# A decoder layer's Z stage fed from x in two layouts: four unscaled fp32 products, column weight and root in one VectorE pass

## The chip, the cores and the metric

The kernel runs on one core of a Trainium2 chip. The metric is the device time of one execution in microseconds (us). PE is TensorE, DVE is VectorE, ACT is ScalarE, POOL is GpSimd, SP is SyncE, which issues most of the DMAs.

## The reference, cut to what matters

One decoder layer on x of 1024 tokens by 1024 columns: an RMS norm, one input projection split into a differential attention group and a gated DeltaNet group, an output projection, and a squared-ReLU MLP. The change lies in the first stage, which computes the norm and the columns of the projection that feed the gate (z) and the decay and write strength (a, b) of the DeltaNet group:

```python
h = rms_norm(x, norm1_w[l])        # x * rsqrt(mean(x*x) + EPS) * w, row by row
proj = h @ w_in[l]
da_q, da_k, da_v, dn_qkv, dn_z, dn_a, dn_b = jnp.split(proj, [...], axis=-1)
...
dn_o = rms_norm(dn_o, dn_out_norm_w[l]) * jax.nn.silu(dn_z.reshape(B, S, DN_HEADS, DN_V_DIM))
```

The later projections use the same h, so the stage also leaves h behind for them.

## The kernel before, in words

**Tiles.** The 1024 tokens are eight blocks of 128, `tb` = 0 to 7. TensorE contracts over partitions, so h is wanted with its columns on partitions: `hH` and `hL` hold h transposed, as eight column blocks `k` of 128 by 1024 tokens. `hH` is h rounded to fp32r and `hL` is what is left, h - hH. The weights are split in the same way (`wH`, `wL`; `z_round` on ACT, `z_rest` on DVE). A product in this split form (`z_mm`, lines 290 to 292) is three matmuls for each `k`: hH wH, hH wL, hL wH, so 24 for one token block and one unit. The Z weights are two units `u` of 260 columns; unit 0 is gate columns, unit 1 is 252 gate columns and the 8 columns of a and b. So the stage has 16 products.

**One block before.** x is loaded as rows (tokens on partitions). ACT squares a block and sums each row (`z_square`, L321); `z_root` takes the root (DVE L223, then a power on POOL, L224); `z_scale` (DVE, L335) multiplies the rows by root and column weight `w1b`; PE transposes the eight column blocks (`z_turn`, L340); ACT copies the result into `hH` (`h_round`, L345) and DVE writes `hL` (`h_rest`, L349). `z_gate` takes a finished product out of PSUM: tanh on ACT (L298), a pass on DVE (L300), a multiplication by `dn_out_norm_w` on POOL (L301), and a store. For block 0 and unit 0 the product is made in plain fp32 from the copied transposes `hF` (L388), before the split forms exist.

`w1b`, the column weight on all partitions, is made by PE from one row (L362).

**What sets the order.** The stage stands in `tc.manual_schedule`: the engines named there take their instructions in the order of the program, each engine for itself. Before, these are PE, DVE and ACT. What stands outside that block (constants, loads, the projections behind it) is placed by a scheduler; the lines between `mark` and `behind.close()` are held behind instructions of the iteration `tb == 3` and behind the last load of x. SP issues the loads.

**Behind the stage** come the DeltaNet projections (`dn_proj`, PE lines 198 to 200). Their weight buffers `wH` and `wL` are those of the Z units, so the first of them is split when the last product of unit 0 is done.

Of the kernel before, what the change touches and what calls it, by code (L numbers as in the profile page):

```python
# [18 lines left out]
P = 128  # L19
# [9 lines left out]
UC = 260  # L29
# [91 lines left out]
def tile_hymba_layer(  # L121
    ctx: ExitStack,
    tc: tile.TileContext,
    x, norm1_w, w_z, w_units, lambda_q1, lambda_k1, lambda_q2, lambda_k2, q_norm_w, k_norm_w,
# [128 lines left out]
    w1b = n1.tile([P, DM], F32, name="w1b")  # L253

    def z_unit(u):

        ops = [staged(t).rearrange("p (k c) -> p k c", k=KB) for t in ("wH", "wL")]
        raws = []
        for k in range(0, KB, 2):
            raw = n1.tile([P, 2 * UC], F32, tag="wraw", name="wraw", bufs=8)  # L260
            nc.sync.dma_start(raw, w_z[u, k // 2, :, 0:2 * UC])
            raws.append(raw.rearrange("p (k c) -> p k c", k=2))
        return ops, raws

    xts = [n1.tile([P, DM], F32, tag="xt", name="xt", bufs=NT) for _ in range(NT)]
    hF = n1.tile([P, KB, P], F32, name="hF")
    w1r = hF.rearrange("p k c -> p (k c)")[0:1, :]
    nc.scalar.dma_start(w1r, norm1_w)
    cuts = (slice(0, 512), slice(512, 1024))
    for c in cuts:  # L270
        nc.sync.dma_start(xts[0][:, c], x2[0:P, c])
    nc.sync.dma_start(xts[1], x2[P:2 * P, :])
    wz = [z_unit(u) for u in range(2)]
    dnw4 = n1.tile([P, 4, P], F32, name="dnw4")
    nc.sync.dma_start(dnw4[:, 0], dn_out_norm_w.partition_broadcast(P))
    for tb in range(2, NT):
        x_last = nc.sync.dma_start(xts[tb], x2[tb * P:(tb + 1) * P, :])
    G.tensor_scalar(dnw4[:, 0], dnw4[:, 0], 0.5, None, ALU.mult)
    G.tensor_copy(dnw4[:, 1:4], dnw4[:, 0:1].broadcast_to([P, 3, P]))
    dnw4 = dnw4.rearrange("p h e -> p (h e)")  # L280

    def z_mm(tb, u, pool=pj, tag="pj", mid=None):
# [4 lines left out]
        for k in range(KB):  # L287
            if k == 2 and mid:
                mid()
            T.matmul(ps[:, :UC], hH[:, k, sl], wh[:, k, :], start=k == 0, stop=False)  # L290
            T.matmul(ps[:, :UC], hH[:, k, sl], wl[:, k, :], start=False, stop=False)
            T.matmul(ps[:, :UC], hL[:, k, sl], wh[:, k, :], start=False, stop=k == KB - 1)
        return ps

    def z_gate(tb, u, ps):
        n = UC if u == 0 else 252
        th = n1.tile([P, UC], F32, tag="zth", name="zth", bufs=2)
        S.activation(th[:, :n], ps[:, :n], AF.Tanh, scale=0.5)  # L298
        zg = n1.tile([P, UC], F32, tag="zg", name="zg", bufs=4)
        last = V.scalar_tensor_tensor(zg[:, :n], th[:, :n], 1.0, ps[:, :n], ALU.add, ALU.mult)  # L300
        G.tensor_tensor(zg[:, :n], zg[:, :n], dnw4[:, UC * u:UC * u + n], ALU.mult)  # L301
        if u == 1:
            last = V.tensor_copy(ab[:, tb, :], ps[:, 252:260])
# [10 lines left out]
    hns_, turned_ = {}, {}  # L314

    def z_square(tb, parts=1):
        hn = n1.tile([P, DM], F32, tag="hn", name="hn", bufs=2)
        ss = n1.tile([P, 2], F32, tag="nss", name="nss", bufs=2)
        for i in range(parts):
            c = cuts[i] if parts > 1 else slice(0, DM)  # L320
            S.activation(hn[:, c], xts[tb][:, c], AF.Square, accum_out=ss[:, i:i + 1])  # L321
        hns_[tb] = hn, ss

    def z_root(tb, parts=1):

        hn, ss = hns_[tb]
        if parts > 1:
            V.tensor_tensor(ss[:, 0:1], ss[:, 0:1], ss[:, 1:2], ALU.add)
        r = n1.tile([P, 1], F32, tag="nr", name="nr", bufs=2)
        rstd(r, ss[:, 0:1], 1.0 / DM, EPS, n1, "nrt", 1)  # L330
        hns_[tb] = hn, r

    def z_scale(tb, c):
        hn, r = hns_[tb]
        return V.scalar_tensor_tensor(hn[:, c], xts[tb][:, c], r, w1b[:, c], ALU.mult, ALU.mult)  # L335

    def z_turn(tb, g):
        ps = pt_.tile([P, 512], F32, tag="pt", name="ps_tr")
        for j in range(4 * g, 4 * g + 4):
            last = T.transpose(ps[:, (j % 4) * P:(j % 4 + 1) * P], hns_[tb][0][:, j * P:(j + 1) * P], ident)  # L340
        turned_[tb, g] = ps.rearrange("p (k t) -> p k t", k=4)
        return last

    def h_round(tb, g):
        return S.copy(hH[:, 4 * g:4 * g + 4, tb * P:(tb + 1) * P], turned_[tb, g])  # L345

    def h_rest(tb, g):
        ks, sl = slice(4 * g, 4 * g + 4), slice(tb * P, (tb + 1) * P)
        V.tensor_tensor(hL[:, ks, sl], turned_[tb, g], hH[:, ks, sl].bitcast(F32), ALU.subtract)  # L349

    ones = gp.tile([P, P], F32, name="ones")
    with tc.manual_schedule(engines={T.engine, V.engine, S.engine}):


        V.memset(ones, 1.0)
        pw = pm.tile([P, 512], F32, tag="pm", name="ps_w")
        for i in range(6):
            T.transpose(pw[:, 0:P], ident, ident)
        pws = []
        for c in cuts:  # L360
            ps = ph.tile([P, 512], F32, tag="ph", name="ps_w1")
            T.matmul(ps, ones[0:1, :], w1r[:, c], start=True, stop=True)  # L362
            pws.append(ps)
        for i in range(6):
            T.transpose(pw[:, 0:P], ident, ident)
        V.tensor_copy(w1b[:, cuts[0]], pws[0])
        z_square(0, 2)
        z_root(0, 2)
        V.tensor_copy(w1b[:, cuts[1]], pws[1])
        z_square(1)  # L370
        for g in range(2):
            z_scale(0, cuts[g])
            z_turn(0, g)
        z_round(0, 0)
        z_root(1)
        S.copy(hF[:, 0:4, :], turned_[0, 0])
        z_rest(0, 0)
        z_round(0, 1)
        S.copy(hF[:, 4:8, :], turned_[0, 1])
        z_scale(1, slice(0, DM))  # L380

        ps = pj.tile([P, 512], F32, tag="pj", name="ps_z")
        banks0 = {0: ps}
        for k in range(KB):
            if k == 4:
                z_turn(1, 0)
                z_turn(1, 1)
            T.matmul(ps[:, :UC], hF[:, k, :], wz[0][1][k // 2][:, k % 2, :], start=k == 0, stop=k == KB - 1)  # L388
        for i in (2, 3):
            z_round(0, i)  # L390
        for i in (1, 2, 3):
            z_rest(0, i)
        for g in range(2):
            h_round(1, g)
            h_rest(1, g)
        for i in range(2):
            z_round(1, i)
            z_rest(1, i)
        for g in range(2):
            ks = slice(4 * g, 4 * g + 4)  # L400
            S.copy(hH[:, ks, 0:P], hF[:, ks, :])
            V.tensor_tensor(hL[:, ks, 0:P], hF[:, ks, :], hH[:, ks, 0:P].bitcast(F32), ALU.subtract)
            z_round(1, 2 + g)
            z_rest(1, 2 + g)
        z_square(2)
        z_root(2)
        banks0[1] = z_mm(1, 0)
        z_gate(0, 0, banks0[0])
        z_scale(2, slice(0, DM))
        z_square(3)  # L410
        banks0[2] = z_mm(0, 1, ph, "ph")
        z_gate(1, 0, banks0[1])
        z_root(3)
        banks0[3] = z_mm(1, 1, ph, "ph", lambda: (z_turn(2, 0), z_turn(2, 1)))
        for g in range(2):
            h_round(2, g)
            h_rest(2, g)
        z_gate(0, 1, banks0[2])
        z_scale(3, slice(0, DM))
        z_gate(1, 1, banks0[3])  # L420
        for tb in range(2, NT):
            ps = z_mm(tb, 0)
            if tb + 1 < NT:
                marks = [z_turn(tb + 1, 0), z_turn(tb + 1, 1)][1:]
                for g in range(2):
                    marks += [h_round(tb + 1, g)]
                    h_rest(tb + 1, g)
            marks += [z_gate(tb, 0, ps)]
            if tb + 2 < NT:
                z_square(tb + 2)  # L430
                z_root(tb + 2)
                z_scale(tb + 2, slice(0, DM))
            if tb == 3:
                mark = marks
            ps = z_mm(tb, 1)
            z_gate(tb, 1, ps)
# [3 lines left out]
    for ins in mark + [x_last]:  # L440
# [3 lines left out]
    tri = sp.tile([P, P], F32, name="tri")  # L444
    G.affine_select(tri, ones, pattern=[[1, P]], compare_op=ALU.is_ge, fill=0.0,
                    base=0, channel_multiplier=-1)
    gt_f = gp.tile([P, P], F32, name="gt_f")
    G.affine_select(gt_f, ones, pattern=[[-1, P]], compare_op=ALU.is_gt, fill=0.0,
                    base=0, channel_multiplier=1)
    gt_r = gp.tile([P, P], F32R, name="gt_r")  # L450
    V.tensor_copy(gt_r, gt_f)
    blk = gp.tile([P, P], F32, name="blk")
    G.affine_select(blk.rearrange("p (b c) -> p b c", c=32), ones.rearrange("p (b c) -> p b c", c=32),
                    pattern=[[-32, 4], [0, 32]], compare_op=ALU.is_ge, fill=0.0,
                    base=-32, channel_multiplier=1)
    caus_f = gp.tile([P, P], F32, name="caus_f")
    G.memset(caus_f, 0.0)
    G.affine_select(caus_f, caus_f, pattern=[[-1, P]], compare_op=ALU.is_ge, fill=-1.0e30,
                    base=0, channel_multiplier=1)
# [103 lines left out]
    def dn_proj(kind):  # L563
        for pr in range(2):
            w = load_unit(w_units[6 + 2 * kind + pr])
# [1223 lines left out]
```

## Time and profile before

| | |
|---|---|
| median of 3 runs | 1257.38 us (1255.05 to 1257.84) |
| the profiled execution | 1254.91 us, span of its instructions 1253.2 us |
| granted TensorE clock, mean | 0.997 |
| busy in the span | PE 98%, its weight loads 85%, DVE 65%, ACT 49%, POOL 9% |
| Z stage on PE | from the first product at 10.02 us to the first projection at 63.45 us |

The durations that the prediction uses come from the profiled execution. In a row of the timeline the first number is the start in us from the span's start, the second the duration in us, then engine, line, operation, tiles written and read, shapes and the count. A bracket gives the idle time of that engine just before, and what ended it. In a row of windows, after the bounds and the length, stand the busy time and the number of instructions of PE, PEld, DVE, ACT and POOL, then the granted clock, the share of the DMA engines and GB/s. Durations overlap with the next instruction on the same engine, so prices are taken from start to start.

### The profile page before, as it was taken

The page shows a single profiled execution, that of the slowest core. Times are in us where ns is not written, and L with a number is a line of the kernel's source. Part 1 is how long each engine was busy: PE and PEld are TensorE (multiplying, and loading weights), DVE is VectorE, ACT ScalarE, POOL GpSimd, SP SyncE. Part 2 cuts the span into 40 slices and gives each one's busy share as a digit, 9 for nine tenths or more (in the row PEclk, how much of TensorE's full clock was granted, in tenths as well). Part 3 has the DMA queues.
Part 4 walks back from the last instruction along what each step waited for, and adds up shares of the span by engine and source line. Part 5 has one row for each costly group of instructions (what it writes and reads, how often), then busy time and mean ns, then how long its engine had stood idle before and what let it go on. Part 6 is the DMA issues. An engine that isn't in the chain of part 4 may idle for free.

```text
span 1253.2 us, 18946 instructions
## 1 busy us (share of the span) xinstructions
PE 1232.7 (98%) x6965; PEld 1061.6 (85%) x6965; DVE 817.7 (65%) x1416; ACT 612.5 (49%) x1239; POOL 111.4 (9%) x143
## 2 busy tenths in 40 slices
PE   9999999999998999999999999999999999999998
PEld 8978888899998998787888888888888888888887
DVE  6567797656556647776589555655569855787553
ACT  5378553334345545656567445445564333333331
POOL 3311110022112200001200000000000000000000
PEclk9999999999999999999999999999999999999999
DMA  7134554368758557322255544443469655422301
GB/s 245 43 102 129 160 159 113 89 215 240 249 144 243 157 176 180 97 66 80 85 185 172 201 159 175 168 152 132 170 219 376 230 199 201 168 101 101 133 35 67
DMA packets 156343, 197.93 MB, mean 158 GB/s; under 512 B 20650, under 2 KB 110554, under 8 KB 156251
## 3 DMA queue, kind: packets, MB, share of 16 engines
q1 hardware_dynamic: 156248, 196.72, 48.4%
q8 instruction: 55, 0.90, 0.3%
q14 instruction: 38, 0.30, 0.1%
q10 hardware_dynamic: 2, 0.00, 0.0%
HBM read 131.66 MB, written 65.01 MB: 157 GB/s over the span
## 4 chain that ended last, share of the span: by engine, by line
PE 91%; DMA 4%; DVE 2%; ACT 2%; issue 1%; SPq 0%; DVEq 0%; POOL 0%; ACTq 0%; POOLq 0%
PE X L1391 5%; PE X L1392 5%; PE X L1393 5%; PE X L1691 4%; PE X L1690 4%; PE X L1689 4%; PE ps_dn L198 3%; PE ps_dn L199 3%; PE ps_dn L200 3%; PE ps_qk L955 3%; PE ps_qk L957 3%; PE ps_qk L956 3%; PE Y L1391 2%; PE Y L1392 2%; PE Y L1393 2%; PE ps_op L1220 2%
## 5 line engine op out<-in xcount | busy, mean ns | idle before, releaser
L1309 ACT CAST hH<-ur 128x1024 fp32r<-128x1024 f32 x56 | 58.9, 1051 | 173.3 <-PE Y L1690 89.8
L1310 DVE TENSOR_TENSOR hL<-ur,hH 128x1024 fp32r<-128x1024 f32 x56 | 68.3, 1223 | 79.9 <-ACT hH L1309 79.8
L955 PE MATMUL ps_qk<-wH,hH 128*128 128x256 f32 x384 | 115.5, 301 | 0.1
L957 PE MATMUL ps_qk<-wH,hL 128*128 128x256 f32 x384 | 109.1, 284 | 0.0
L956 PE MATMUL ps_qk<-wL,hH 128*128 128x256 f32 x384 | 109.0, 284 | 0.0
L1310 DVE TENSOR_TENSOR op<-raw,op 128x1024 fp32r<-128x1024 f32 x48 | 58.7, 1223 | 74.5 <-PE X L1392 41.5
L1689 PE MATMUL X<-hH 128*128 128x512 f32 x224 | 87.1, 389 | 0.0
L1690 PE MATMUL X<-hL,hH 128*128 128x512 f32 x224 | 87.1, 389 | 0.0
L1691 PE MATMUL X<-hH,hL 128*128 128x512 f32 x224 | 87.1, 389 | 0.0
L198 PE MATMUL ps_dn<-hH,wH 128*128 128x512 f32 x192 | 76.1, 397 | 0.3 <-ACT cp L574 0.3
L200 PE MATMUL ps_dn<-hH,wL 128*128 128x512 f32 x192 | 75.9, 396 | 0.0
L199 PE MATMUL ps_dn<-hL,wH 128*128 128x512 f32 x192 | 75.7, 395 | 0.0
L955 PEld LDWEIGHTS ps_qk<-wH,hH 128*128 128x128 f32 x384 | 74.0, 193 | 0.3 <-ACT qn L974 0.2
L956 PEld LDWEIGHTS ps_qk<-wL,hH 128*128 128x128 f32 x384 | 74.0, 193 | 0.0
L957 PEld LDWEIGHTS ps_qk<-wH,hL 128*128 128x128 f32 x384 | 73.8, 192 | 0.0
L193 DVE TENSOR_TENSOR wL<-wraw,wH 128x512 fp32r<-128x512 f32 x64 | 43.9, 697 | 37.9 <-ACT wH L192 37.7
L1310 DVE TENSOR_TENSOR hL<-dw,hH 128x1024 fp32r<-128x1024 f32 x56 | 68.1, 1219 | 0.5 <-ACT hH L1309 0.5
L1309 ACT CAST op<-raw 128x1024 fp32r<-128x1024 f32 x48 | 50.4, 1051 | 35.3 <-PE Y L1393 19.9
L1309 ACT CAST hH<-dw 128x1024 fp32r<-128x1024 f32 x56 | 58.7, 1048 | 10.1 <-DMA dw<-in_w_down_dram 4.4
L192 ACT CAST wH<-wraw 128x512 fp32r<-128x512 f32 x64 | 38.2, 620 | 48.7 <-DMA wraw<-in_w_units_dram 35.3
L578 DVE SCALAR_TENSOR_TENSOR cy<-cp,pv,cy 128x512 f32<-128x512 f32 x72 | 53.7, 747 | 7.2 <-ACT cy L576 6.4
L1080 DVE TENSOR_REDUCE mx<-ps_sc 128x1 f32<-128x128 f32 (+7 forms) x64 | 47.6, 754 | 15.3 <-PE ps_sc L1078 14.8
(366 smaller groups left out, 3451.3 us busy)
## 6 DMA issues: line engine op xcount, KB each, us to landing
ur<-ud SPq DMA_DIRECT2D x28, 1024.0 KB, 4.9
raw<-in_w_up_dram SPq DMA_DIRECT2D x32, 512.0 KB, 4.1
dw<-in_w_down_dram SPq DMA_DIRECT2D x32, 512.0 KB, 6.6
wraw<-in_w_units_dram SPq DMA_DIRECT2D x48, 256.0 KB, 3.9
qk_d<-qa SPq DMA_DIRECT2D x32, 256.0 KB, 3.6
ud<-ua SPq DMA_DIRECT2D x16, 512.0 KB, 3.3
ud<-s SPq DMA_DIRECT2D x16, 512.0 KB, 2.7
pka<-park_d SPq DMA_DIRECT2D x32, 192.0 KB, 3.7
```

Of the source, the lines that this page charges most:

```text
L198: T.matmul(ps, lh(k), rh(k), start=(k == 0), stop=False)
L199: T.matmul(ps, lh(k), rl(k), start=False, stop=False)
L200: T.matmul(ps, ll(k), rh(k), start=False, stop=(k == n - 1))
L955: T.matmul(ps[:, :256], hH[:, k, sl], wh[:, k, :], start=(k == 0), stop=False)
L956: T.matmul(ps[:, :256], hH[:, k, sl], wl[:, k, :], start=False, stop=False)
L957: T.matmul(ps[:, :256], hL[:, k, sl], wh[:, k, :], start=False, stop=(k == KB - 1))
L1309: S.copy(dst[0], src)
L1310: V.tensor_tensor(dst[1], src, dst[0].bitcast(F32), ALU.subtract)
L1391: T.matmul(ps, op[0][:, k, cs], h[0][:, k, :], start=start and k == 0, stop=False, skip_group_check=True)
L1689: T.matmul(bank[t], v[0][:, j, sl], v[2][:, j], start=s0, stop=False, skip_group_check=True)
L1690: T.matmul(bank[t], v[0][:, j, sl], v[3][:, j], start=False, stop=False, skip_group_check=True)
L1691: T.matmul(bank[t], v[1][:, j, sl], v[2][:, j], start=False, stop=s1, skip_group_check=True)
```

## The change: what it does

- **x comes in two layouts.** The host hands over `x_cols`, where each token block already has columns on partitions, beside x itself. Each block is loaded twice: as `xT` for the products, and as rows `xt` for the squares alone. The transposes on PE are gone.
- **Four unscaled products.** The products of blocks 0 and 1 with both units are made in plain fp32 from `xT` times the column weight (`z_weigh`, then `z_raw`), without the root. Their root is applied in `z_gate`: as the scale of the tanh, and in an additional DVE pass which also takes the place of the POOL multiplication.
- **The root is spread by PE.** ACT scales the identity by a block's roots (`z_diag`), and PE multiplies ones by that diagonal (`z_spread`), so that each partition holds the roots of all 128 tokens. `z_spread` stands inside a product, ahead of column block `at`.
- **Column weight and root in one DVE pass.** `z_scale` multiplies `xT` by the column weight and the spread roots, straight from PSUM, in eight passes of 128x128 (blocks 2 to 7) or two of 128x512 with the roots alone (blocks 0 and 1, weighted before), then writes `hH` and `hL`. Blocks 0 and 1 get theirs late, in the iterations 4 and 5.
- **Order.** Loads and roots are reordered; POOL is now also in manual order, its masks ahead of the stage. The first loads of the projections' weights stand behind the last load of x.

The diff, cut to its core:

```diff
+    def z_raw(tb, u, pool, tag, mid=None, at=2):
+        ps = pool.tile([P, 512], F32, tag=tag, name="ps_z")
+        for k in range(KB):
+            if k == at and mid is not None:
+                z_spread(mid)
+            T.matmul(ps[:, :UC], xTs[tb][:, k, :], wz[u][1][k // 2][:, k % 2, :], start=k == 0, stop=k == KB - 1)
+        return ps
...
-        S.activation(th[:, :n], ps[:, :n], AF.Tanh, scale=0.5)
+        S.activation(th[:, :n], ps[:, :n], AF.Tanh, scale=half_r[tb] if raw else 0.5)
         last = V.scalar_tensor_tensor(zg[:, :n], th[:, :n], 1.0, ps[:, :n], ALU.add, ALU.mult)
-        G.tensor_tensor(zg[:, :n], zg[:, :n], dnw4[:, UC * u:UC * u + n], ALU.mult)
+        if raw:
+            last = V.scalar_tensor_tensor(zg[:, :n], zg[:, :n], r, w, ALU.mult, ALU.mult)
+        else:
+            G.tensor_tensor(zg[:, :n], zg[:, :n], w, ALU.mult)
...
+    def z_weigh(tb):
+        for c in cuts:
+            V.tensor_tensor(xTs[tb][:, c, :], xTs[tb][:, c, :], w1c[:, c].unsqueeze(2).broadcast_to([P, 4, P]),
+                            ALU.mult)
+    def z_diag(tb):
+        diags[tb] = n1.tile([P, P], F32, tag="dg", name="dg", bufs=4)
+        S.activation(diags[tb], ident, AF.Copy, scale=roots[tb])
+    def z_spread(tb):
+        ps = pm.tile([P, 512], F32, tag="pm", name="ps_r")
+        marks[tb] = T.matmul(ps[:, :P], ones, diags[tb], start=True, stop=True)
+        spreads[tb] = ps[:, :P]
+    def z_scale_parts(tb):
+        sl = slice(tb * P, (tb + 1) * P)
+        xT, last = xTs[tb], []
+        for c in cuts:
+            if tb < 2:
+                V.tensor_tensor(xT[:, c, :], xT[:, c, :], spreads[tb].unsqueeze(1).broadcast_to([P, 4, P]), ALU.mult)
+            else:
+                for k in range(c.start, c.stop):
+                    V.scalar_tensor_tensor(xT[:, k, :], xT[:, k, :], w1c[:, k:k + 1], spreads[tb], ALU.mult, ALU.mult)
+            last.append(S.copy(hH[:, c, sl], xT[:, c, :]))
+        yield
+        for c in cuts:
+            last.append(V.tensor_tensor(hL[:, c, sl], xT[:, c, :], hH[:, c, sl].bitcast(F32), ALU.subtract))
+        yield last
...
+        z_weigh(0)
+        z = {(0, 0): z_raw(0, 0, pj, "pj")}
+        for i in range(3):
             z_round(0, i)
             z_rest(0, i)
+        z_weigh(1)
+        z_round(0, 3)
+        z_rest(0, 3)
+        z[1, 0] = z_raw(1, 0, pj, "pj")
+        for i in range(4):
             z_round(1, i)
             z_rest(1, i)
         z_square(2)
         z_root(2)
+        z_diag(2)
+        z[0, 1] = z_raw(0, 1, ph, "ph", 2, 6)
         z_square(3)
         z_root(3)
+        z_diag(3)
+        z[1, 1] = z_raw(1, 1, ph, "ph", 3, 4)
+        z_scale(2)
+        z_square(0)
+        z_square(1)
+        parts = z_scale_parts(3)
+        next(parts)
+        for tb in range(2):
+            z_root(tb)
+        next(parts)
+        ...
+        z_square(4)
+        ...
+        z[2, 0] = z_mm(2, 0, pt_, "pt")
+        z_gate(0, 0, z[0, 0], True)
+        z_root(4)
+        z_diag(4)
+        z_gate(1, 0, z[1, 0], True)
+        z_gate(0, 1, z[0, 1], True)
+        z[2, 1] = z_mm(2, 1, pt_, "pt", 4, 6)
+        z_scale(4)
+        z_square(5)
+        z_gate(2, 0, z[2, 0])
+        z_root(5)
+        z_diag(5)
+        z_gate(1, 1, z[1, 1], True)
+        z_gate(2, 1, z[2, 1])
+        for tb in range(3, NT):
+            late = tb - 4 if 4 <= tb < 6 else None
+            z[tb, 0] = z_mm(tb, 0, mid=late)
+            if late is not None:
+                z_scale(late)
+            z[tb, 1] = z_mm(tb, 1, mid=tb + 2 if tb + 2 < NT else None)
+            z_gate(tb, 0, z[tb, 0])
             if tb + 2 < NT:
+                last = z_scale(tb + 2)
+                if tb == 3:
+                    mark = [marks[5], *last]
+            if tb + 3 < NT:
+                z_square(tb + 3)
+                z_root(tb + 3)
+                z_diag(tb + 3)
+            if 3 <= tb < 5:
+                z_diag(tb - 3)
+            z_gate(tb, 1, z[tb, 1])
...
-            w = load_unit(w_units[6 + 2 * kind + pr])
+            with tc.issue_after(x_last.ins) if kind == 1 and pr == 0 else ExitStack():
+                w = load_unit(w_units[6 + 2 * kind + pr])
```

The loads on SP stand in this order: the first half of `xT` 0, the first quarter of unit 0, the second half of `xT` 0, the rest of unit 0, `xT` 1, unit 1, then `xT` and x of blocks 2 and 3, `dn_out_norm_w`, x of blocks 0 and 1, then `xT` and x of blocks 4 to 7. `xT` has six buffers, `xt` four.

More of the change, by code (lines that the diff above doesn't have):

```diff
@@ L312, in z_rest @@
         V.tensor_tensor(wl, wz[u][1][i], wh.bitcast(F32), ALU.subtract)
[L314 to L345, printed above, removed]
@@ L347, in h_rest @@
[L347 to L355 removed]
+    sums, roots, half_r, spreads, diags = {}, {}, {}, {}, {}
+    def z_weigh(tb):
+        for c in cuts:
+            V.tensor_tensor(xTs[tb][:, c, :], xTs[tb][:, c, :], w1c[:, c].unsqueeze(2).broadcast_to([P, 4, P]),
+                            ALU.mult)
@@ new lines, in z_square, with z_root @@
+    def z_square(tb):
+        sq = n1.tile([P, DM], F32, tag="sq", name="sq", bufs=1)
+        ss = n1.tile([P, 1], F32, tag="nss", name="nss", bufs=4)
+        S.activation(sq, xts[tb], AF.Square, accum_out=ss)
+        sums[tb] = ss
+    def z_root(tb):
+        r = roots[tb] = n1.tile([P, 1], F32, name=f"nr{tb}")
+        rstd(r, sums[tb], 1.0 / DM, EPS, n1, "nrt", 1)
+    def z_diag(tb):
+        diags[tb] = n1.tile([P, P], F32, tag="dg", name="dg", bufs=4)
+        S.activation(diags[tb], ident, AF.Copy, scale=roots[tb])
@@ new lines, in z_scale @@
+    def z_scale(tb):
+        return list(z_scale_parts(tb))[1]
+    ones = gp.tile([P, P], F32, name="ones")
+    V.memset(ones, 1.0)
+    tri = sp.tile([P, P], F32, name="tri")
+    gt_f = gp.tile([P, P], F32, name="gt_f")
+    blk = gp.tile([P, P], F32, name="blk")
+    caus_f = gp.tile([P, P], F32, name="caus_f")
+    G.memset(caus_f, 0.0)
+    G.affine_select(caus_f, caus_f, pattern=[[-1, P]], compare_op=ALU.is_ge, fill=-1.0e30,
+                    base=0, channel_multiplier=1)
+    G.affine_select(tri, ones, pattern=[[1, P]], compare_op=ALU.is_ge, fill=0.0,
+                    base=0, channel_multiplier=-1)
@@ L356, in tile_hymba_layer @@
+    G.affine_select(gt_f, ones, pattern=[[-1, P]], compare_op=ALU.is_gt, fill=0.0,
+                    base=0, channel_multiplier=1)
+    G.affine_select(blk.rearrange("p (b c) -> p b c", c=32), ones.rearrange("p (b c) -> p b c", c=32),
+                    pattern=[[-32, 4], [0, 32]], compare_op=ALU.is_ge, fill=0.0,
+                    base=-32, channel_multiplier=1)
+    marks = {}
+    with tc.manual_schedule(engines={T.engine, V.engine, S.engine, G.engine}):
         pw = pm.tile([P, 512], F32, tag="pm", name="ps_w")
-        for i in range(6):
+        for i in range(10):
@@ L358, in tile_hymba_layer @@
             T.transpose(pw[:, 0:P], ident, ident)
[L359 to L388, printed above, removed]
@@ new lines, in tile_hymba_layer @@
+        z[1, 1] = z_raw(1, 1, ph, "ph", 3, 4)
[7 more added lines that the diff above has]
+        next(parts)
+        for tb in range(2):
+            half_r[tb] = n1.tile([P, 1], F32, name=f"hr{tb}")
+            V.tensor_scalar(half_r[tb], roots[tb], 0.5, None, ALU.mult)
+        z_square(4)
+        G.tensor_scalar(dnw4[:, 0], dnw4[:, 0], 0.5, None, ALU.mult)
+        G.tensor_copy(dnw4[:, 1:4], dnw4[:, 0:1].broadcast_to([P, 3, P]))
```

128 lines of the change are left out of this document (49 added, 79 removed).

## The prediction

> **What bounds the kernel now.** I read the page first: the engines' shares, then the chain that ended last, to see which engine's time is the kernel's time.
>
> ```profile
> span 1253.2 us, 18946 instructions
> PE 1232.7 (98%) x6965; PEld 1061.6 (85%) x6965; DVE 817.7 (65%) x1416; ACT 612.5 (49%) x1239; POOL 111.4 (9%) x143
> PE 91%; DMA 4%; DVE 2%; ACT 2%; issue 1%; SPq 0%; DVEq 0%; POOL 0%; ACTq 0%; POOLq 0%
> ```
>
> PE holds 91% of that chain. So a change in the Z stage moves the end by as much as it moves the moment at which PE starts the first projection behind it. Then the windows of the stage and PE's timeline at its seams (start, duration, engine, line):
>
> ```profile
> 0.00:10.00 10.00, 8.46 (x24) 5.01 (x24) 4.05 (x12) 4.90 (x10) 2.96 (x13) 1.00 0.77 268
> 14.40:63.45 49.05, 49.05 (x412) 48.63 (x411) 29.91 (x65) 21.34 (x48) 16.77 (x23) 1.00 0.29 102
> 8.23 1.97 PE L340 MATMUL ps_tr<-ident,hn 128*128 128x128 f32 x8
> 11.99 1.04 PE L340 MATMUL ps_tr<-ident,hn 128*128 128x128 f32 x8
> 12.87 1.92 PE L388 MATMUL ps_z<-wraw,hF 128*128 128x260 f32 x8
> 14.43 0.47 PE L290 MATMUL ps_z<-wH,hH 128*128 128x260 f32 x1
> 23.06 0.28 PE L292 MATMUL ps_z<-wH,hL 128*128 128x260 f32 x1
> 23.18 0.28 PE L290 MATMUL ps_z<-wH,hH 128*128 128x260 f32 x1
> 63.45 0.40 PE L198 MATMUL ps_dn<-hH,wH 128*128 128x512 f32 x1
> ```
>
> The stage ends on PE at 63.45 us, and from 14.4 on PE never waits (49.05 busy of 49.05). Starts give the prices: a split product is 24 matmuls 0.12 us apart (23.06, 23.18), 2.87 us. An unscaled one has two PE instructions for each of its 8 blocks: eight take 12.87 to 14.43, nearly 0.44 us a block, 3.5 us in all. Eight transposes take 0.87 us (11.99 to 12.87). The same eight at 8.23 take twice as long: early in the kernel PE runs at half speed, which the clock column does not show.
>
> **The ideal sum, if nothing waits.** Three more products unscaled: 3 x (3.5 - 2.87) = +1.9 us. Out go 64 transposes, eight groups of 0.87, -7.0. In come eight fp32 products of ones and a diagonal, two instructions each, which I take as two transposes of that size, 0.22, and 0.08 for the change of form: +2.4. PE's first product starts when half a block of x has landed (3.54 below) and one DVE pass of 0.69 has weighted it, 4.3 instead of 10.0; at half speed to about 10.3 and with its weights still landing, it ends near 10.9. Then 3 x 3.5 + 12 x 2.87 + 8 x 0.30 = 47.3: 58.2 us, a gain of 5.3. What the ideal assumes is that each diagonal is ready when PE comes to it, because the spread product stands inside a z product on PE, and all behind it waits.
>
> **Every engine keeps the written order.** The block for tb = 3 before, DVE, ACT and POOL:
>
> ```profile
> 29.00 1.07 ACT L321 ACTIVATE hn<-xt 128x1024 f32<-128x1024 f32 x1
> 29.95 0.21 ACT L321 ACTIVATION_READ_ACCUMULATOR hn<-xt 128x1 f32 x1
> 54.60 1.07 ACT L345 CAST hH<-ps_tr 128x512 fp32r<-128x512 f32 x2 [2.92 <-PE ps_tr L340]
> 31.07 0.38 ACT L298 ACTIVATE zth<-ps_z 128x252 f32<-128x252 f32 x1 [0.92 <-PE ps_z L292]
> 28.38 1.29 DVE L349 TENSOR_TENSOR hL<-ps_tr,hH 128x512 fp32r<-128x512 f32 x2 [2.61 <-ACT hH L345]
> 30.25 0.15 DVE L223 TENSOR_SCALAR nrt<-nss 128x1 f32<-128x1 f32 x1
> 30.47 0.75 POOL L301 TENSOR_TENSOR zg<-zg,dnw 128x260 f32<-128x260 f32 x1 [3.82 <-DVE nrt L223]
> 31.18 0.55 POOL L224 TENSOR_TENSOR nr<-nrt,neghalf 128x1 f32<-128x1 f32 x1
> 31.76 1.29 DVE L335 SCALAR_TENSOR_TENSOR hn<-xt,nr,w1b 128x1024 f32<-128x1024 f32 x1 [1.36 <-POOL nr L224]
> 32.96 0.41 DVE L300 SCALAR_TENSOR_TENSOR zg<-zth,ps_z 128x252 f32<-128x252 f32 x1
> 33.29 0.16 DVE L303 COPY ab<-ps_z 128x8 f32<-128x8 f32 x1
> 91.63 1.12 DVE L676 SCALAR_TENSOR_TENSOR lt<-ps_m,small,dtm 128x128 f32<-128x128 f32 x4
> 92.66 0.68 DVE L681 TENSOR_TENSOR kn<-ps_t,kds 128x512 f32<-128x512 f32 x1
> 73.54 1.28 ACT L629 ACTIVATE rrh<-tri,gghr 128x128 fp32r<-128x128 f32 x4 [1.13 <-DVE gghr L530]
> ```
>
> DVE stood idle for a root until 31.76 though the tanh for its next instruction was done at 31.45; that one ran only at 32.96. A wait holds everything written behind it. Prices, from start to start: DVE pass of 128x512 0.60, gate pass 0.33 (32.96 to 33.29), scalar_tensor_tensor of 128x128 out of PSUM 0.26 (four from 91.63 to 92.66); ACT copy 0.48, square with its sum 1.04, tanh 0.3, a diagonal 0.3 to 0.4 (nearest: L629, four in 1.28); POOL gate 0.7, root 0.55. For tb >= 2 the new z_scale is 8 x 0.26 + 2 x 0.60 = 3.3 us on DVE, where before it was 1.2 + 1.2.
>
> **The three waits.** Loads first:
>
> ```profile
> 3.54 0.63 ACT L321 ACTIVATE hn<-xt 128x512 f32<-128x512 f32 x1 [0.90 <-DMA xt<-in_x_dram]
> 2.54 5.27 SPq L261 DMA_DIRECT2D wraw<-in_w_z_dram  x8
> DMA to landing us min/median/max: 5.4/6.4/6.4
> 8.85 3.73 SPq L277 DMA_DIRECT2D xt<-in_x_dram  x6
> 15.00:20.00 5.00, 5.00 (x45) 5.00 (x44) 4.64 (x9) 4.48 (x10) 1.84 (x3) 1.00 1.00 403
> 36.53 0.22 DVE L443 CAST identb<-ident 128x128 bf16<-128x128 f32 x1
> 38.08 0.27 DVE L483 TENSOR_REDUCE lams<-lamp 128x2 f32<-128x128 f32 x1
> ```
>
> Two blocks of x and all z weights land by about 7.5 + 5.4 = 12.9 before. The same bytes are first in line after; I take 11.4 to 12.8, as SP no longer spends 0.77 us on one early load. At 403 GB/s a 512 KB block takes 1.3 us; xT2, x2, xT3, x3 follow, so x3 lands at 16.6 (to 18.0). From there, estimates by these prices in written order:
>
> 1. Square 3 ends 17.75, and DVE's root step for block 3 stands ahead of z_scale(2): DVE starts block 2 at 17.85, has blocks 2 and 3 done at 24.8, gate (0,0) at 26.2; root and diagonal 4 are ready at 27.3. PE comes there at 27.0: 0.4 us.
> 2. Diagonal 5: gates (1,0) and (0,1) on DVE (tanh behind diagonal 4 on ACT) to 29.05; eight passes to 31.1; copy to 31.8, square 32.8, tanh 33.2, gate and root step 33.6, POOL gate then root 34.95, diagonal 35.4. PE between spread 4 and spread 5 has 0.3 + 0.72 + 2.87 + 0.72 = 4.6 us of work and is there at 32.0: wait 3.4.
> 3. Diagonal 0 stands behind square 6 and diagonal 6 on ACT, though its own root is old: gates to 37.15, eight passes 39.25, copy 39.9, square 41.0, root 41.85, two diagonals 42.55. PE has 0.3 + 2.15 + 0.72 = 3.2 us between spread 5 and spread 0: wait 4.0. The constants released at this point (identb to lams, 36.53 to 38.35) can stand before that root step: up to 1.3 more.
> 4. Diagonal 1, the same way: gate (3,1) 43.25, block 0 and gate (4,0) 46.2, block 6 48.3, square 7 50.1, diagonals 51.6. PE between spread 6 and spread 1 again 3.2: wait 2.8.
>
> From 51.7, PE has 0.3 + 2.15 + 2.87 + 0.3 + 4 x 2.87 = 17.1: end 68.7, with the constants 70.1; I take 69.4, +5.95 against 63.45.
>
> **PE's clock after a wait.** It is shown once, far from here:
>
> ```profile
> 398.35 0.28 PE L957 MATMUL ps_qk<-wH,hL 128*128 128x256 f32 x1
> 401.33 0.33 PE L920 MATMUL ps_qkt<-ident,qn 128*128 128x128 f32 x1 [2.70 <-ACT at L1118]
> 402.80:406.20 3.40, 3.40 (x19) 3.40 (x18) 2.42 (x5) 0.79 (x3) 0.80 (x1) 0.50 0.67 222
> 367.90:369.50 1.60, 0.30 (x4) 0.10 (x2) 1.18 (x4) 1.59 (x4) 0.00 (x0) 1.00 0.59 174
> 369.50:373.00 3.50, 3.50 (x29) 3.41 (x30) 2.48 (x9) 1.75 (x7) 1.01 (x1) 1.00 0.67 156
> ```
>
> A gap of 2.98 us was followed by 3.4 us at granted clock 0.50; one of 1.6 us was not. Half clock for 3.4 us costs 1.7. Behind waits 2 and 3 much of that is inside the next wait; behind the last it is not. I count one: +1.7, and keep 0 and 3.4 as ends.
>
> The Trainium skill, "TensorE: Matmul & The Clock Gate", section What's actually happening, drops the clock after one idle window of about 3.4 us. By that rule alone the last wait, 2.8, would not drop it, and the sum would be +6 and not +7.7; the 2.98 us gap above dropped it, and the measurement decides.
>
> **What I cost at nothing.** w1b's two products and copies and the transposes of the opening go; they lay before 10 us. Eight more loads on SP at about 0.65 us of queue each (8.85 to 12.21 for six), 5 us: behind them stand the gate stores (seven buffers) and the constants' loads, needed after 36 us, and the first two projection weights, now behind the last x, needed at 61 us or later; if x's buffers came free late, the projection would start late instead. The POOL masks move ahead of the stage and ran at 0.9 to 2.5 already. Four POOL gate passes become DVE passes, 4 x 0.33, counted above.
>
> **Sum.** 5.95 + 1.7 = +7.7 on the profiled execution's 1254.91: 1262.6. The median of the runs is 2.5 above that execution, which would give 1265.0. I say 1264.
>
> **Rivals.**
> - Faster: the waits are not there, since the chain of roots keeps ahead of PE. Place: diagonals 5, 0 and 1. It decides when each chain is shorter than PE's 4.6, 3.2 and 3.2 us. Then 58.2, -5.3: about 1251. For it: DVE is busy 29.9 of 49 us before. Against it: with no queueing at all, spread 5 to diagonal 0 is 8 passes 2.1, copy 0.6, square 1.1, root 0.8, two diagonals 0.7, latencies 0.5: 5.8 over 3.2. 0.11.
> - No change: waits add up to about 5 us, half of mine, if the loads come 1.5 us earlier and the clock holds. 1257. 0.09.
> - Slower still: DVE and POOL slow each other, or loads of x in two layouts (4.2 MB more, 10.4 us at 403 GB/s) bring x3 at 18 or later and the copied blocks late; 2 to 3 us at each wait and a clock drop behind two: +14, 1270 or above. 0.12.
> - My forecast, +3 to +12: 0.68.
>
> The range 1257 to 1271 leaves out the faster case, and little at the top. What measurement can tell from no change here is about 0.2%, 2.5 us: faster 0.11, same 0.10, slower 0.79.
>
> **What the profile after would show.** PE's first product near 4.3; unscaled products 0.44 us a block; PE waiting in the spread matmul for ACT's diagonal at blocks 5, 0 and 1, 2.5 to 5 us each; granted clock 0.50 in a window before 60 us; the first ps_dn near 71. Wrong if ps_dn starts before 63: then the diagonals were in time, or the order on ACT is not the written one. Right in place but wrong in size if the waits are there and DVE's 128x128 passes are not 0.26.

## The result, and the profile after

The changed kernel takes 1264.26 us, median of 4 runs (1262.67 to 1265.15), against 1256.86 for the kernel before on the same chip (4 runs, 1255.05 to 1257.84): ratio 1.0059, 95% interval 1.0042 to 1.0077. Timed again with more runs (e10) the ratio was 1.0072, 1.0051 to 1.0093. It is slower by some 0.6%, little but clear of the scatter. The profiled execution took 1262.67 us.

First the page, span, shares and chain:

```profile
span 1261.0 us, 18863 instructions
PE 1229.8 (98%) x6887; PEld 1058.9 (84%) x6887; DVE 826.1 (66%) x1466; ACT 617.4 (49%) x1243; POOL 107.7 (9%) x139
PE 89%; DMA 4%; DVE 3%; ACT 2%; issue 1%; SPq 1%; POOL 0%; DVEq 0%; ACTq 0%; POOLq 0%
```

PE has 3 us less to do (1229.8 for 1232.7) in a span that is 7.8 longer, so the loss is idle time of PE (time at half clock counts as busy here). PE's part of the waits of the first 75 us says for what (what waited, for what; total, times, longest), and the timeline of the spread products and of the seam says where (cut: the spreads of blocks 3 and 7, which do not wait, are left out):

```profile
PE ps_r L377 <- ACT dg L372: 11.6, 5, 4.2
```

```profile
4.61 11.83 PE L322 MATMUL ps_z<-wraw,xT 128*128 128x260 f32 x44 [0.68 <-DVE xT L355]
16.70 0.49 PE L377 MATMUL ps_r<-dg,ones 128*128 128x128 f32 x2 [0.26 <-ACT dg L372]
...
28.98 0.76 PE L377 MATMUL ps_r<-dg,ones 128*128 128x128 f32 x2 [2.17 <-ACT dg L372]
37.63 0.49 PE L377 MATMUL ps_r<-dg,ones 128*128 128x128 f32 x2 [2.31 <-ACT dg L372]
45.54 0.49 PE L377 MATMUL ps_r<-dg,ones 128*128 128x128 f32 x2 [4.17 <-ACT dg L372]
50.27 0.38 PE L377 MATMUL ps_r<-dg,ones 128*128 128x128 f32 x2
56.23 0.70 PE L377 MATMUL ps_r<-dg,ones 128*128 128x128 f32 x2 [2.70 <-ACT dg L372]
...
74.80 0.40 PE L198 MATMUL ps_dn<-hH,wH 128*128 128x512 f32 x1
```

The order is that of the spreads: blocks 2, 3, 4, 5, 0, 6, 1, 7. PE stands at blocks 4, 5, 0 and 1, each time for ACT's diagonal; the fifth wait, 0.26 us at block 2, is small. The first projection starts at 74.80, 11.35 us later than before (63.45). The windows of the stage (PE's busy time stands second, the granted clock third from the end):

```profile
27.00:35.00 8.00, 6.02 (x37) 6.02 (x38) 5.93 (x18) 3.40 (x8) 0.57 (x1) 0.79 0.52 180
35.00:45.00 10.00, 4.06 (x30) 3.45 (x28) 7.10 (x29) 4.50 (x13) 3.21 (x5) 1.00 0.42 139
28.90:32.40 3.50, 3.42 (x16) 3.42 (x17) 3.01 (x10) 0.84 (x4) 0.00 (x0) 0.52 0.46 173
46.10:49.50 3.40, 3.40 (x18) 3.40 (x17) 2.66 (x6) 1.22 (x2) 0.72 (x1) 0.50 0.13 43
56.30:59.80 3.50, 3.50 (x17) 3.50 (x18) 3.07 (x6) 1.35 (x3) 0.72 (x1) 0.51 0.11 37
```

From 35 to 45 us PE works 4.06 us of 10, where before it never stopped. The last three rows are three stretches at half clock, each of which costs half its 3.4 us. The prediction's ideal stage of 58.2 us, plus 11.6 of waits, plus 3 x 1.7, is 74.9; measured 74.80.

The stage loses 11.35 us and the span only 7.8, so the rest of the kernel took 3.6 us less. The windows from the first projection to the end, before and after:

```profile
63.45:1253.17 1189.72, 1170.78 (x6510) 1004.04 (x6508) 779.69 (x1336) 582.48 (x1175) 91.60 (x107) 1.00 0.49 159
```

```profile
74.80:1260.97 1186.17, 1168.80 (x6510) 1002.21 (x6508) 780.07 (x1336) 583.07 (x1175) 91.46 (x107) 1.00 0.50 159
```

The same 6510 PE instructions stand in both. Before, the trace's clock record has two half-clock stretches here (402.8 and 583.7), after none. Whether this is the work of the change or chance is asked in e7, e8 and e10.

### The profile page after: what moved, and what is told of

Its sections match the earlier page's. It is cut to its first block, busy times and chain, and to the rows that moved or that the text cites. A ratio compares the mean times of both kernels' runs of the same rounds, so it can differ in the third digit from the quotient of the medians.

```text
span 1261.0 us, 18863 instructions
## 1 busy us (share of the span) xinstructions
PE 1229.8 (98%) x6887; PEld 1058.9 (84%) x6887; DVE 826.1 (66%) x1466; ACT 617.4 (49%) x1243; POOL 107.7 (9%) x139
## 4 chain that ended last, share of the span: by engine, by line
PE 89%; DMA 4%; DVE 3%; ACT 2%; issue 1%; SPq 1%; POOL 0%; DVEq 0%; ACTq 0%; POOLq 0%
PE X L1428 5%; PE X L1429 5%; PE X L1430 5%; PE X L1728 4%; PE X L1727 4%; PE X L1726 4%; PE ps_dn L198 3%; PE ps_dn L200 3%; PE ps_dn L199 3%; PE ps_qk L992 3%; PE ps_qk L994 3%; PE ps_qk L993 3%; PE Y L1428 2%; PE Y L1429 2%; PE Y L1430 2%; PE ps_op L1257 2%
## 5 line engine op out<-in xcount | busy, mean ns | idle before, releaser
L198 PE MATMUL ps_dn<-hH,wH 128*128 128x512 f32 x192 | 76.2, 397 | 0.2 <-ACT cp L611 0.2
L1346 ACT CAST hH<-dw 128x1024 fp32r<-128x1024 f32 x56 | 58.7, 1049 | 10.7 <-DMA dw<-in_w_down_dram 5.0
L1121 ACT ACTIVATE pexp<-ps_sc,mx 128x128 f32<-128x128 f32 (+7 forms) x64 | 47.3, 740 | 20.0 <-DVE mx L1117 19.9
```

Of the source, the lines that this page charges most:

```text
L198: T.matmul(ps, lh(k), rh(k), start=(k == 0), stop=False)
L1346: S.copy(dst[0], src)
```

## The experiments

Theory A: PE waits because in the written order each diagonal stands behind work that is not needed so soon, and every engine keeps that order; moving it gives the time back. Theory B: VectorE's added work (eight passes of 0.26 us instead of one of 1.2, two passes for a raw gate) sets the pace in any order. Theory C, for the 3.6 us: the change makes what follows the stage faster. (In the texts put down for e1 to e3, C is another rival: that the loads of x in two layouts set the pace.)

**e1: the diagonals of blocks 0 and 1 early.** The first edits also give the diagonals eight buffers instead of four.

```diff
             V.tensor_scalar(half_r[tb], roots[tb], 0.5, None, ALU.mult)
+        for tb in range(2):
+            z_diag(tb)
...
-            if 3 <= tb < 5:
-                z_diag(tb - 3)
```

> Edit: the changed kernel with the diagonals of blocks 0 and 1 made on ACT right after their roots, ahead of square 4, instead of behind the diagonals of blocks 6 and 7. Theory A (PE waits in the spread products, because each diagonal stands behind other work in ACT's written order): the waits at spread 0 (4.2 us) and spread 1 (2.7 us) go, about 0.9 us each comes up at spreads 6 and 7, the clock stays up behind them, and the first projection starts at 66 to 67 instead of 74.8 us; the time falls by 7 to 9 us. Rival B (the loss is the work: longer unscaled products and the eight 128x128 DVE passes): the stage still ends above 73. Rival C (the loads of x in two layouts set the pace): the waits move to other places and the stage ends within 1 us of 74.8.

1261.95 us, ratio to before 1.0049 (1.0032 to 1.0065); first projection at 72.06. PE's waits:

```profile
PE ps_r L377 <- ACT dg L372: 6.5, 3, 3.7
PE ps_z L311 <- DVE ab L340: 3.8, 3, 2.4
```

The waits at blocks 0 and 1 are gone, 6.9 us of them, but only 2.7 us came out at the end. Block 4's wait grew from 2.17 to 3.66 us: the two early diagonals stand ahead of square 4 on ACT and hold it until 26.3 us, and the profile puts another 0.57 us there down to the load of x. A new wait appeared too: products wait for a PSUM bank that a gate still has to read. The place was right, the size a miss.

**e2: squares, roots and diagonals of blocks 4 to 7 ahead of gates and scales.**

```diff
-        z_gate(0, 0, z[0, 0], True)
         z_root(4)
         z_diag(4)
+        z_gate(0, 0, z[0, 0], True)
+        z_square(5)
+        z_root(5)
+        z_diag(5)
...
+            if tb + 3 < NT:
+                z_square(tb + 3)
+                z_root(tb + 3)
+                z_diag(tb + 3)
             z[tb, 1] = z_mm(tb, 1, mid=tb + 2 if tb + 2 < NT else None)
```

(The same lines behind `z_scale` go.)

> Edit: the changed kernel with square, root and diagonal of blocks 4 and 5 ahead of the gates, and in the loop those of block tb+3 ahead of z_scale(tb+2); the diagonals of blocks 0 and 1 stay where they were. Theory A: the wait at spread 5 goes, that at spread 4 falls from 2.2 to about 1.5 (x of block 4 lands at 25.1), spread 0 and 1 still wait for copies, 2 to 3.7 us; first projection at about 65. B: above 73. C: the wait at spread 5 does not go, since x of block 5 lands at 27.2 only; above 73.

1260.92 us, 1.0044 (1.0029 to 1.0059); first projection at 70.78. Again a new wait takes over. PE's waits, then ACT and DVE around it:

```profile
PE ps_z L311 <- DVE zg L331: 5.8, 1, 5.8
PE ps_r L377 <- ACT dg L372: 3.7, 4, 1.4
```

```profile
39.88 0.40 ACT L372 ACTIVATE dg<-ident,nr 128x128 f32<-128x128 f32 x1 [1.44 <-POOL nr L224]
40.18 0.37 ACT L330 ACTIVATE zth<-ps_z 128x260 f32<-128x260 f32 x1
40.58 0.42 DVE L331 SCALAR_TENSOR_TENSOR zg<-zth,ps_z 128x260 f32<-128x260 f32 x1 [1.89 <-ACT zth L330]
```

The tanh of block 3, unit 0, stands behind a diagonal that waits 1.44 us for POOL's root; its bank comes free when DVE has ended the gate's pass at 41.0, and the product that needs that bank has stood since 35.2. In the last of these microseconds each engine was idle for another: ACT for POOL, DVE for ACT, PE for DVE. The wait at spread 5 is gone though the loads are the same, which speaks against the loads; theory A's 65 us was missed by 6.

**e3: both.**

> Edit: both of the edits above. Theory A: only spread 4 waits (about 1.5 us), and perhaps the product of block 7 for its DVE pass (under 1 us); first projection at 60 to 61 us, before the 63.4 of the kernel before, and a time 2 to 4 us under it. B and C: at or above the kernel before.

1261.19 us, 1.0044 (1.0031 to 1.0056); first projection at 70.49. The forecast of a time under the kernel before was far off. What waits is no longer the diagonal:

```profile
PE ps_z L311 <- DVE zg L331: 6.9, 2, 5.8
PE ps_r L377 <- ACT dg L372: 2.1, 2, 1.7
PE ps_z L311 <- DVE ab L340: 1.1, 2, 0.6
```

This outcome is what theory B would give as well: moving diagonals alone does not tell A and B apart.

**e4: transposes in the waits, to keep the clock.** Results go to a part of the bank that nothing reads.

```diff
+        for _ in range({4: 16, 5: 18, 0: 34, 1: 22}.get(tb, 0)):
+            T.transpose(ps[:, P:2 * P], ident, ident)
         marks[tb] = T.matmul(ps[:, :P], ones, diags[tb], start=True, stop=True)
```

> Edit: the changed kernel with transposes of the identity on PE right before the spreads of blocks 4, 5, 0 and 1 (16, 18, 34 and 22 of them), into a free part of the spread's bank; they take a little less than the waits and compute nothing that is used. If the clock drops cost time: granted clock 1.00 through the whole stage; the drop behind spread 4 is hidden by the next wait, those behind spread 0 and spread 1 are not, so the first projection starts at about 71.5 instead of 74.8. If they are hidden by the waits: 74.8 as before. If PE is the bound: later than 74.8.

First projection at 72.53, with one half-clock stretch in the stage, where none was expected, instead of three: 2.3 us sooner than in the first profile of the changed kernel, 1.1 to 3.2 sooner than in its three. The time, 1265.31 us (1264.94 to 1266.02), is not lower: in the profiled run four stretches fell behind the stage. The half clock is worth a couple of us in the stage, then; the larger part of the loss is the waits themselves.

**e6: less work on VectorE, order unchanged.** Blocks 2 to 7 are scaled in two 128x512 passes by the root alone; the column weight is left out there.

```diff
-                for k in range(c.start, c.stop):
-                    V.scalar_tensor_tensor(xT[:, k, :], xT[:, k, :], w1c[:, k:k + 1], spreads[tb], ALU.mult, ALU.mult)
+                V.tensor_tensor(xT[:, c, :], xT[:, c, :], spreads[tb].unsqueeze(1).broadcast_to([P, 4, P]), ALU.mult)
```

> The changed kernel in its own order, with the eight one-pass column-weight-and-root instructions of blocks 2 to 7 (2.16 us a block) replaced by two 128x512 passes with the spread roots alone (about 1.4 us a block): the column weight is left out for those blocks. Theory A (order): the chain behind each late diagonal is mostly ScalarE and POOL steps; waits fall by 0 to 0.8 us each at blocks 4, 5, 0 and 1, first ps_dn at 72 to 75. Theory B (VectorE's work sets the pace): six blocks by 0.8 us, and the gates freed with it, take 5 us or more off, first ps_dn at 67 to 70.

One run, 1259.46 us; first projection at 72.13. Square 4 on ACT, and the waits on the diagonals of blocks 4, 5, 0 and 1:

```profile
25.50 1.06 ACT L361 ACTIVATE sq<-xt 128x1024 f32<-128x1024 f32 x1 [1.66 <-DMA xt<-in_x_dram]
29.28 0.49 PE L377 MATMUL ps_r<-dg,ones 128*128 128x128 f32 x2 [2.30 <-ACT dg L372]
37.06 0.49 PE L377 MATMUL ps_r<-dg,ones 128*128 128x128 f32 x2 [1.47 <-ACT dg L372]
44.11 0.79 PE L377 MATMUL ps_r<-dg,ones 128*128 128x128 f32 x2 [3.31 <-ACT dg L372]
55.10 0.49 PE L377 MATMUL ps_r<-dg,ones 128*128 128x128 f32 x2 [1.83 <-ACT dg L372]
```

The waits at blocks 5, 0 and 1 fell from 2.31, 4.17 and 2.70 us by 0.84, 0.86 and 0.87: about the 0.8 us by which the pass in each chain got shorter, and no more. Block 4's did not fall (2.30 after 2.17): ACT stood 1.66 us for x of block 4, so there the load holds the chain up. That fits theory A; B's 67 to 70 was not reached.

**e5: the whole stage in another order, arithmetic unchanged.** Each of the chains square, root, diagonal stands well ahead of its spread; a raw gate is cut in two, so that the tanh and the DVE pass that read the bank come first and the pass with the root and the store later; blocks 0 and 1 get their scale in the iterations 6 and 7; x of block 4 is loaded ahead of the gate's weights, x0 and x1. The diff is cut:

```diff
         z_scale(2)
+        z_square(4)
+        z_root(4)
+        z_diag(4)
+        z_scale(3)
...
+        z_gate_a(0, 0, z[0, 0], True)
+        z_square(5)
+        z_gate_a(1, 0, z[1, 0], True)
+        z_root(5)
+        z_diag(5)
+        z_gate_b(0, 0, True)
...
-            late = tb - 4 if 4 <= tb < 6 else None
+            late = tb - 6 if tb >= 6 else None
```

> The changed kernel with the same arithmetic, and its Z stage written in another order: square, root and diagonal of blocks 4, 5, 6, 7, and of 0 and 1, stand well ahead of their spreads; each raw block's gate is split so that the tanh and the pass that read the PSUM bank come first and the pass with the row's root and the store come later; blocks 0 and 1 get their scale in blocks 6 and 7's turn; x of block 4 is loaded ahead of dnw, x0 and x1. Theory A (only the written order makes TensorE wait; the arithmetic per block fits behind 6.2 us of products): the waits on diagonals and on gates' banks fall from 11.6 us to under 3, the first ps_dn instruction stands at 59 to 62 us and the time is 1250 to 1254 us, under the kernel before. Theory B (VectorE's and ScalarE's work per block is itself what sets the pace once the waits on diagonals are gone): the waits move again to banks or to hH/hL, first ps_dn stays at 67 to 72, time 1258 to 1262.

1255.74 us against 1254.91, ratio 1.0007 (0.9996 to 1.0019): no difference from the kernel before. First projection at 63.44, no wait on a diagonal left. Theory A's figures (59 to 62, 1250 to 1254) were a little too good, B's (67 to 72, 1258 to 1262) are out. Two waits for banks remained, and a half-clock stretch behind the second (58.2 + 3.4 + 1.7 = 63.3):

```profile
29.00 0.39 PE L315 MATMUL ps_z<-wH,hH 128*128 128x260 f32 x1 [0.98 <-DVE zg L337]
42.49 0.39 ACT L336 ACTIVATE zth<-ps_z 128x260 f32<-128x260 f32 x1 [0.34 <-DVE zg L337]
43.97 0.59 PE L315 MATMUL ps_z<-wH,hH 128*128 128x260 f32 x1 [2.39 <-DVE zg L337]
```

The tanh at 42.49 is that of block 4, unit 0: three older gates had been written ahead of it, behind block 5's scale, while only two banks served the products of blocks 3 to 7.

**e9: those two waits taken up.** The squares and roots of blocks 0 and 1 stand between block 3's passes; gates (2,0) and (1,1) ahead of block 5's scale; the products of blocks 4 to 6 take turns in six banks. The diff shows the banks alone, against e5:

```diff
+        where = {(4, 0): (ph, "ph"), (5, 0): (ph, "ph"), (6, 0): (pt_, "pt"), (6, 1): (pt_, "pt")}
         for tb in range(4, NT):
             late = tb - 6 if tb >= 6 else None
-            z[tb, 0] = z_mm(tb, 0, mid=late)
+            z[tb, 0] = z_mm(tb, 0, *where.get((tb, 0), (pj, "pj")), mid=late)
```

> The order of e5, with the two waits that e5 left taken up: the squares of blocks 0 and 1 stand between block 3's ScalarE passes, their roots between its VectorE passes, so that the first raw gate frees its bank sooner; the gates (2,0) and (1,1) stand ahead of block 5's scale; the products of blocks 4 to 6 take turns in six PSUM banks instead of two. Arithmetic as in the changed kernel. Theory A (order alone): e5's waits of 1.2 and 2.4 us on gates' banks and the half-clock stretch behind the second (1.7) go; first ps_dn at 58 to 60.5, time 1249 to 1253, at least 3 us under the kernel before. Theory B (the vector work sets the pace, e5 already stands at its bound): first ps_dn 62 to 65, time 1254 to 1258.

1250.25 us (10 runs, 1248.12 to 1252.38) against 1254.64 (15 runs): ratio 0.9961, interval 0.9948 to 0.9975. It beats both kernels: the changed one took 1263.76 beside it (e10), 13.5 us more, and its first projection starts 13.5 us later (73.61). PE's waits, its seam, and the windows:

```profile
PE ps_z L315 <- DVE zg L337: 1.0, 1, 1.0
PE ps_r L390 <- ACT dg L385: 0.6, 1, 0.6
```

```profile
60.14 0.50 PE L198 MATMUL ps_dn<-hH,wH 128*128 128x512 f32 x1 [0.72 <-DVE zg L337]
```

```profile
35.00:45.00 10.00, 10.00 (x86) 10.00 (x85) 8.63 (x34) 5.12 (x15) 4.33 (x7) 1.00 0.49 157
45.00:55.00 10.00, 10.00 (x84) 9.80 (x83) 9.79 (x30) 5.49 (x13) 2.60 (x4) 1.00 0.16 54
```

Where the changed kernel's PE worked 4.06 us of 10, it now works all 10, at full clock, with the same instructions per block. So the arithmetic fits behind the products; theory B falls, though not by much: DVE is busy 9.79 of 10 us from 45 to 55. What gave the time back is the order, the split gates, the earlier load of block 4 and the six banks together; no run parts them.

**e7, e8 and e10: both kernels again, unchanged.**

> The changed kernel unchanged, profiled once more. Theory A (the half-clock stretches fall where an idle gap meets a free-running 3.4-us window, so those behind the Z stage come and go from run to run): first ps_dn again at 74 to 75.5; the stretches behind 80 us may number 0 to 3, and span less first ps_dn is 1186.2 plus about 1.7 for each. Theory C (the change itself, through a better order behind the Z stage, takes 3.6 us off the rest): no stretch behind 80 us, and span less first ps_dn 1186.0 to 1186.6 again.

> The kernel before unchanged, profiled once more. Theory A (half-clock stretches behind the Z stage come by the phase of a free-running window): first ps_dn at 63.2 to 63.8 and span less first ps_dn 1186.2 plus about 1.7 for each stretch, whose number may differ from the two seen. Theory C (the rest of the kernel is slower before than after): two stretches again at the same places and 1189.4 to 1190.0.

> The changed kernel unchanged, timed in five rounds against the kernel before. Theory A (what the Z stage loses is the whole difference; half-clock stretches behind it fall by chance in both kernels): the difference of the medians is 10 to 13 us, first ps_dn 74 to 76. Theory C (the change gives 3 to 4 us back behind the Z stage): the difference of the medians is 6.5 to 8.5 us and span less first ps_dn is 1186 to 1187.

The windows from the first projection to the end: the changed kernel in e7, the kernel before in e8, the changed kernel in e10.

```profile
75.71:1266.16 1190.45, 1170.28 (x6510) 1003.43 (x6508) 780.90 (x1336) 583.01 (x1175) 91.46 (x107) 1.00 0.49 159
```

```profile
63.76:1251.36 1187.60, 1169.14 (x6510) 1002.62 (x6508) 780.23 (x1336) 582.77 (x1175) 91.65 (x107) 1.00 0.49 159
```

```profile
73.61:1261.09 1187.48, 1170.65 (x6510) 1004.32 (x6508) 780.56 (x1336) 583.52 (x1175) 91.64 (x107) 1.00 0.49 159
```

The rest of the changed kernel took 1186.2, 1190.5 and 1187.5 us, that of the kernel before 1189.7 and 1187.6. In e1 to e6 and e9, whose code behind the stage is the same, it took 1185.6 to 1191.8; the ten profiles with x in two layouts average 1188.2, the two of before 1188.7. So the 3 to 4 us of theory C are not there, and the 3.6 us of the first pair lie within the scatter of single profiles. Half-clock stretches are part of that scatter (0, 1 and 2 of them after; 2 and 1 before; PE's busy time in the rest goes from 1168.80 to 1170.8), but they do not order it: by theory A's 1186.2 plus 1.7 a stretch, e7 with one should take 1187.9 and e10 with two 1189.6. Idle time inside the rest, from 16.8 to 20.2 us, varies as well; what moves it from run to run stays open.

The changed kernel's stage ends at 74.80, 75.71 and 73.61, the other's at 63.45 and 63.76: 11.1 us apart on the mean. The timed medians of e10 are 9.1 us apart (1263.76 and 1254.64), below the 10 to 13 that A expected and above C's 6.5 to 8.5. Its ratio allows 6.4 to 11.7: it holds 11.1, but the first pair's 5.3 to 9.7 does not. That remaining 2 us or so was not settled.

## Why the prediction was right, point by point

**Right: what bounds the stage.** "What the ideal assumes is that each diagonal is ready when PE comes to it." The ideal of 58.2 us held: with the measured waits and half-clock stretches added it gives the end of the stage in e5 (63.3 for 63.44), in e9 (58.2, 0.6 on the first diagonal, 1.0 on a bank and 0.7 at the seam make 60.5, for 60.14), and in all three profiles of the changed kernel (e7: 58.2 + 11.2 + 4 x 1.7 = 76.2 for 75.71; e10: 58.2 + 11.2 + 2 x 1.7 = 72.8 for 73.61). Such sums test the term for the work, to within 0.8 us; waits and clock are put in as measured. The first product started at 4.61 (forecast 4.3), the eight passes take 2.15 us (8 x 0.26 = 2.1).

**Right in place and in sum: the waits.** About 11 us forecast with the constants (0.4, 3.4, 4.0 and 2.8, and 0.65 for the middle of the constants' share), 11.6 measured. Of the four sizes two were off, in opposite directions, so the agreement of the sum is in part luck. Block 4 was 2.17, not 0.4. The rows of ACT and DVE there:

```profile
25.19 1.06 ACT L361 ACTIVATE sq<-xt 128x1024 f32<-128x1024 f32 x1 [0.70 <-DMA xt<-in_x_dram]
27.28 0.49 DVE L334 SCALAR_TENSOR_TENSOR zg<-zg,nr,dnw 128x260 f32<-128x260 f32 x1
27.69 0.15 DVE L223 TENSOR_SCALAR nrt<-nss 128x1 f32<-128x1 f32 x1
28.52 0.40 ACT L372 ACTIVATE dg<-ident,nr 128x128 f32<-128x128 f32 x1 [1.82 <-POOL nr L224]
```

x of block 4 landed at 25.1, which the prediction's walk had not followed, and the raw gate's second pass is 0.49 and starts 0.54 behind the first, where the walk took 0.33 for it. Block 5 was 2.31, not 3.4: its diagonal came 2.2 us later than forecast, PE 3.3 us later. Block 0's wait (4.17 for 4.0 to 5.3) followed the forecast chain, with the constants (from identb on) ahead of the root step:

```profile
42.39 1.05 ACT L361 ACTIVATE sq<-xt 128x1024 f32<-128x1024 f32 x1
43.12 0.22 DVE L493 CAST identb<-ident 128x128 bf16<-128x128 f32 x1
43.98 0.15 DVE L223 TENSOR_SCALAR nrt<-nss 128x1 f32<-128x1 f32 x1
44.79 0.69 ACT L372 ACTIVATE dg<-ident,nr 128x128 f32<-128x128 f32 x2 [0.17 <-POOL nr L224]
```

Block 1's was 2.70 for 2.8.

**Mis-sized: the clock.** "I count one: +1.7, and keep 0 and 3.4 as ends." There were three in the first profile, four in e7 (two of them back to back), two in e10: 3.4 to 6.8 us. In the first profile this is 3.4 of the 3.7 us by which the stage lost more than forecast (11.35 for 7.7). The prediction took those behind waits 2 and 3 to lie inside the next wait. For a stretch ahead of block 5's or block 0's wait the runs agree. In the first profile one lies behind block 4 (29.05); in e10 the clock stays full there and PE waits 3.86 us at block 5 instead of 2.31, then a stretch follows (37.91) and the wait at block 0 is 2.67 instead of 4.17:

```profile
38.02 0.80 PE L377 MATMUL ps_r<-dg,ones 128*128 128x128 f32 x2 [3.86 <-ACT dg L372]
45.94 0.49 PE L377 MATMUL ps_r<-dg,ones 128*128 128x128 f32 x2 [2.67 <-ACT dg L372]
```

The one behind wait 3 (46.12) is not hidden so: spread 6 (50.27) stands in PE's order behind the slowed products, and the chain of block 6's scale, square 7 and diagonal 1 starts from it. With it spread 1 starts 10.7 us behind spread 0 (56.23 and 45.54), in e10 without it 9.15 (55.09 and 45.94), and the wait at spread 1 is 2.70 in both. A half-clock stretch ahead of a spread from which the next diagonal's chain starts delays the chain with PE. The prediction's own example was also shorter than it says: 2.98 us runs from start to start, and the gap's row has 2.70 of idle time.

**Right by chance: the step from the stage to the whole.** The stage lost 11.35 us, not 7.7; that the profiled execution came out at 1262.67 beside a sum of 1262.6 is because 3.6 us fell away behind the stage, which the scatter of the rest (1185.6 to 1191.8) covers. The change's mechanism and sign were as forecast; the total agrees better than its terms, and the first ps_dn, forecast near 71, came at 73.6 to 75.7.

**The rivals.** "The chain of roots keeps ahead of PE" did not happen in this order, but e9 shows that it can, at 60.14 and 1250.25, close to that rival's 58.2 and 1251. The argument against it, "5.8 over 3.2", holds only while a diagonal's square starts behind the scale of the block before. "No change" needed waits of about 5 us; there were 11.6. "Slower still" was not seen: x3's load was in time, and only block 4's was late.

## What to carry to other kernels

When every engine keeps a written order, a chain of four steps on three engines (square on ACT, DVE's and POOL's steps of the root, diagonal on ACT) has to be written well ahead of its use. Here moving one such chain alone handed most of the wait to whatever then stood behind it: PSUM banks that wait for a gate. Look for the oldest reader of a resource that is standing behind something younger, split a step where its first half frees the resource, and give the products more banks than the gates are late. Busy shares are a first hint whether it is order or work: DVE was busy 7.1 of the 10 us in which PE worked 4.06.

## What the runs showed of the hardware that was not expected

**Half clock follows a fixed grid, not the length of a gap.** In the trace's clock record of each run, all half-clock stretches start at the same phase of a 3.4133 us grid, within 0.01 us (e7: 30.24, 43.90, 57.55 and 415.95, each 2.94 modulo 3.4133), and last one, two or three times 3.41; the phase differs between runs of the same kernel (0.06 and 1.02 before; 1.75, 2.94 and 0.37 after). Where the grid cuts a gap decides. The same gap of about 3 us in the changed kernel, PE's row and the window behind it, in the first profile and in e10:

```profile
412.80 0.33 PE L957 MATMUL ps_qkt<-ident,qn 128*128 128x128 f32 x1 [2.85 <-ACT at L1155]
412.90:416.30 3.40, 3.40 (x30) 3.40 (x31) 3.18 (x8) 2.15 (x6) 0.00 (x0) 1.00 0.52 148
```

```profile
409.87 0.43 PE L957 MATMUL ps_qkt<-ident,qn 128*128 128x128 f32 x1 [3.09 <-ACT at L1155]
410.00:413.40 3.40, 3.40 (x17) 3.40 (x18) 3.18 (x8) 2.25 (x6) 0.00 (x0) 0.50 0.42 123
```

In the first, the grid cut the gap into 1.40 and 1.45 us of two windows, and the clock stayed full; in e10 one window held all 3.09, and the next ran at half clock. In the twelve profiles no window that was idle for more than 1.75 us was followed by full clock; most that dropped had 1.8 to 3.4 idle, though eight dropped with 0.8 to 1.6, three of these while the clock was half already. A wait of 2 us is thus enough if one window holds it.

The Trainium skill, "TensorE: Matmul & The Clock Gate", section What's actually happening, states such a free-running window of 3413 ns, and the traces agree to the hundredth. It also lets the clock fall after one idle window; here a window somewhat over half idle was enough, and the measurement decides.
